# Down-projection passes of a fused GLA and MLP kernel: two of a round's three new column passes begin with a step by sums, and the last round has one more

## The chip, the cores and the metric

The kernel runs on one core of a Trainium2 chip. The time is that of one execution on the device, in microseconds (us), taken as the median of several runs. A lower time is better. One further execution is recorded by the hardware profiler, and the rows quoted here come from that one.

## The reference, cut to what matters

The trunk has one layer: a chunked gated linear attention (GLA) with a residual, then an MLP with squared ReLU and a residual, then a final RMSNorm. There are 256 tokens, a model width of 2048 and a hidden width of 8192, all in float32. The change touches the MLP alone:

```
h = h + gla_mixer(rmsnorm(h))
a = relu(rmsnorm(h) @ w_up)          # 256 x 2048 @ 2048 x 8192
h = h + (a * a) @ w_down             # 256 x 8192 @ 8192 x 2048
out = rmsnorm(h) * final_norm
```

## The kernel before

**Precision.** TensorE multiplies fp32r operands. Every float32 operand is split into two: `hi` is the rounded copy, made on ScalarE (ACT, `copy_hi`, L118), and `lo` is the rest, made on VectorE (DVE, a subtraction, L131, L154 or L943). A block product is three matmuls: hi by hi, hi by lo and lo by hi.

**The MLP.** The 8192 hidden rows are worked through in eight rounds `m` (0 to 7) of 1024. In a round, `up` makes 1024 hidden activations, and `down` multiplies them with the matching rows of `w_down`, in column groups `g` of 512 (four of them; the last round has only groups 0 and 1 here, and the other half of its columns is left to the loop at the end of the kernel). One column group in one round is a *column pass*, and a pass has four steps `kp` of 256 rows. `order_of` reverses the order of the groups each round, so the first pass of a round goes on with the group that ended the round before, and its accumulators stay where they are. The other three passes of a round are new column passes: the code calls them `fresh`.

**Two ways of a step.** A down step is a 2 by 2 by 2 product of blocks (two halves of the tokens, two of the 256 rows, two of the 512 columns). The *direct* way makes all 8 block products, 24 matmuls of 256 columns, into two accumulators, B32 and BX4. The way *by sums* (Strassen's, in Winograd's form) makes 7 block products, 21 matmuls, into four accumulators, P16, B32, P57 and BX4. It needs sums of weight blocks: three additions on DVE (L914) into `work`, one more `hi` (two copies of 128x512, L118) and one more `lo` of 128x1024 (L943), in slots of their own; of the weights themselves only three of four blocks are split (128x768 in place of 128x1024). It also needs sums of the activations, S1 to S4, which `forms` (L801) makes and `form_parts` (L811, L812) splits. `by_sums(m, g, kp)` says which way a step goes; `ways_of` collects over all groups which of the two a `kp` needs, and so how much `forms` and `form_parts` make.

**Accumulators and banks.** There are eight PSUM banks. A down pass holds four, an up half-round two, and when one up half-round follows another, the old pair is released only when DVE has normalised it (`normalized`, L786, called by `start`). Between passes an accumulator lives in SBUF: P16 and P57 in `sums`, B32 and BX4 in `h`. `begin(k, g)` takes a bank and copies the home into it; `settle(k)` copies the former pass's bank to its home and releases it; both are ACT copies of 128x512 (`copy_end`, L827). At the end of a pass, `ahead` begins B32 and BX4 of the next one in the two free banks. A fresh pass makes its step 0 the direct way, which needs only those two. P16 is settled and begun in step `first` (its first step by sums, step 1), P57 after that step's first products, and B32 and BX4 of the former pass are settled at the step's end.

**Order of the work.** The instructions are issued alternately: half an up step, half a down step. One up step and one down step together are called a *unit* below; a round has 16, so unit 0 to 3 is its first pass and units 4, 8 and 12 begin the fresh ones. `up` runs 18 steps ahead. The order is fixed on all three engines: `in_order` chains TensorE's products; on ACT each `copy_hi` and `copy_end` follows the one before it (L116 to L118, L823 to L827); on DVE the additions follow the newest `lo`, and a `lo` follows the newest additions. In a unit by sums ACT's order is: `hi` of the down weights, `hi` of the up weights, two `hi` of the sums. DVE's is: `lo` of the down weights, the additions, `lo` of the up weights, `lo` of the sums. The work on activations (`normalized`, `forms`, `form_parts`) is put in between by `piece`, one closure after each up step. There are five `hi` and `lo` slots and six raw weight tiles (`slots`, `raw_tile`).

Of the kernel before, what the change touches and what calls it, by code (L numbers as in the profile page):

```python
# [68 lines left out]
def tile_gla_mlp(ctx, tc, x, xt, cols, w_vg, w_in, w_gate, w_out, w_up, w_down, final_norm, out):  # L69
# [12 lines left out]
    def psum_bank(i, name="acc"):  # L82
        return psum.tile([P, 512], F32, tag=f"b{i}", name=name)
# [19 lines left out]
    def flush():  # L103
        while side:
            side.popleft()()
# [6 lines left out]
    def copy_hi(to, raw):  # L112
        with ExitStack() as order:
            if last_end[0]:
                order.enter_context(tc.issue_after(last_end[0]))
            if ordered[0]:  # L116
                order.enter_context(tc.issue_after(last_hi[0].ins))
            last_hi[0] = nc.scalar.copy(to, raw)  # L118
# [102 lines left out]
    g1 = lambda kt: colt[:, kt : kt + 1]  # L221
# [265 lines left out]
    at = big.tile([P, 2, HEADS, 3 * P + 64], F32R, tag="C", name="at")  # L487
# [179 lines left out]
    def order_of(m):  # L667

        return range(GROUPS)[:: 1 if m % 2 else -1]

    def by_sums(m, g, kp):

        if m == ROUNDS - 1:
            return g < 2 and kp == 2
        if m == ROUNDS - 2 and g == order_of(m)[-1]:
            return kp == 1
        return kp > 0 or m > 0 and g == order_of(m)[0]


    LEAD = KT + 2  # L680
# [16 lines left out]
    def matmul(o, x, w, first, last):  # L697
        newest[0] = nc.tensor.matmul(o, x, w, start=first, stop=last, skip_group_check=True).ins  # L698
# [123 lines left out]
    def copy_end(to, src):  # L822

        with tc.issue_after(last_hi[0].ins), ExitStack() as order:
            if last_end[0]:
                order.enter_context(tc.issue_after(last_end[0]))
            last_end[0] = nc.scalar.copy(to, src).ins  # L827
# [8 lines left out]
    P16, B32, P57, BX4 = range(4)  # L836

    def home(k, g):
        if k in (P16, P57):
            return sums[g][:, 1:3] if k == P16 else sums[g][:, 0::3]  # L840
        return h[:, k // 2, g * GT : (g + 1) * GT].rearrange("p (f s) -> p f s", f=2)
# [3 lines left out]
    def begin(k, g):  # L845
        i = free.popleft()
        bank = psum_bank(i)
        if k in (B32, BX4) or g in begun:
            copy_end(two(bank), home(k, g))
            used.add(bank.name)  # L850
        return i, bank
# [9 lines left out]
    def settle(*ks):  # L861

        for k in ks:
            late.pop(k, lambda: None)()

    def down(passes):

        ahead = pending = None
        units = 0
        for n, (m, g) in enumerate(passes):
            fresh = not n or passes[n - 1][1] != g
            if fresh:
                banks = ahead or {k: begin(k, g) for k in (B32, BX4)}
                if m == ROUNDS - 1:
                    flush()
            ends = n + 1 == len(passes) or passes[n + 1][1] != g
            first = min(kp for kp in range(KP) if by_sums(m, g, kp)) if fresh else None  # L880
            for kp in range(KP):
                last = ends and kp == KP - 1
                by_parts = by_sums(m, g, kp)

                def products(n, these, w, banks=banks, last=last):

                    with in_order():
                        for k, o, a, c in these:
                            bank = banks[k][1]
                            for x in a[: 2 - n]:  # L890
                                for d in range(0, c.stop - c.start, T):
                                    matmul(
                                        bank[:, o + d : o + d + T], x, w[n][:, c.start + d : c.start + d + T],
                                        bank.name not in used, last and n == 1,
                                    )
                                    used.add(bank.name)

                raw = raw_tile()[:, : 2 * GT]
                c0 = m * MR + 2 * kp * P
                src = w_down[c0 : c0 + 2 * P, g * GT : (g + 1) * GT].rearrange("(i p) c -> p i c", p=P)  # L900
                last_load[0] = nc.sync.dma_start(out=raw.rearrange("p (i c) -> p i c", i=2), in_=src)
                w = parts(raw, 2 * GT, slots(), [(T * by_parts, 2 * GT)])
                if fresh and kp == first:
                    settle(P16)
                    banks[P16] = begin(P16, g)
                at = lambda f, m=m, kp=kp: stationary(m, kp, f)
                block = lambda i, n=1: slice(i * T, (i + n) * T)
                if by_parts:
                    these = (P16, 0, at(A11), block(1)), (B32, T, at(A12), block(3)), (B32, 0, at(S4), block(2))
                    wk = work[:, n_sums[0] % 2]  # L910
                    n_sums[0] += 1
                    u = wk.rearrange("p (f s) -> p f s", f=4)
                    raw = raw.rearrange("p (f s) -> p f s", f=4)
                    add = lambda o, x, y: nc.vector.tensor_tensor(o, x, y, op=ALU.add)  # L914

                    with tc.issue_after(last_lo[0].ins):
                        add(u[:, :2], raw[:, :1].to_broadcast([P, 2, T]), raw[:, 1:3])
                        add(u[:, 2], u[:, 0], raw[:, 2])
                        last_sum[0] = add(u[:, 3], u[:, 2], raw[:, 3]).ins
                else:  # L920
                    these = [
                        (k, 0, at(f[i]), block(2 * i, 2))
                        for i in range(2) for k, f in ((B32, (A11, A12)), (BX4, (A21, A22)))
                    ]
                for part in range(2):
                    products(part, these, w)
                if pending:
                    for _ in pending:
                        pass
                    pending = None  # L930
                yield
                if fresh and kp == first:
                    settle(P57)
                    banks[P57] = begin(P57, g)

                def of_sums(wk=wk if by_parts else None, products=products, at=at):


                    to = slots()
                    for c in (0, GT):  # L940
                        copy_hi(to[0][:, c : c + GT], wk[:, c : c + GT])
                    with tc.issue_after(last_lo[0].ins):
                        last_lo[0] = nc.vector.tensor_tensor(to[1][:, :G], wk, to[0][:, :G].bitcast(F32), op=ALU.subtract)  # L943
                    early = (P57, 0, at(S1), block(0)), (P57, T, at(S3), block(1))
                    late = (P16, T, at(S2), block(2)), (BX4, T, at(A22), block(3))
                    products(0, early, to)
                    yield
                    products(0, late, to)
                    products(1, (*early, *late), to)

                alone = units + LEAD >= UPS
                if by_parts:
                    if alone:

                        pending = of_sums()
                    else:
                        rest = of_sums()
                        next(rest)
                yield
                if by_parts and not alone:  # L960
                    next(rest, None)
                units += 1
                if last:
                    if n + 1 < len(passes):
                        ahead = {k: begin(k, passes[n + 1][1]) for k in (B32, BX4)}
                    else:
                        last_banks(0)
                if fresh and kp == first:
                    settle(B32, BX4)
            if ends:  # L970

                def end(k, i, bank, g=g):
                    copy_end(home(k, g), two(bank))
                    free.append(i)

                late.update({k: lambda k=k, end=end, of=banks[k]: end(k, *of) for k in range(4)})
                begun.add(g)
                if m == ROUNDS - 1 or m == ROUNDS - 2 and g > 1:
                    late[BX4] = lambda f=late[BX4], g=g: (f(), side.extend(combine(g)))
# [15 lines left out]
    passes = [(m, g) for m in range(ROUNDS) for g in order_of(m) if m < ROUNDS - 1 or g < 2]  # L995
# [4 lines left out]
    for _ in down(passes):  # L1000
        next(steps, None)
# [34 lines left out]
    for kt in range(KL):  # L1036
        k = kt - KL + ROOM
# [87 lines left out]
```

## Time and profile before

| | |
|---|---|
| median of 3 runs | 1058.89 us (1058.55 to 1059.53) |
| profiled execution, its own time | 1059.51 us |
| its span | 1057.5 us, so 2.0 us lie around the span |
| TensorE (PE) busy | 1048.8 us, 9160 matmuls |
| DVE busy | 822.9 us |
| ACT busy | 693.7 us |
| a round from unit 4 to the next round's unit 4 (618.27 to 700.97) | 82.70 us: PE 82.70, DVE 76.05, ACT 62.35 |

A busy time is a union over an engine's instructions. Matmuls are pipelined, so one lasts 276 ns in the rows while the next starts about 113 ns later. DVE instructions overlap by about 0.08 us, so the distance between two starts, not the duration, is what one costs. In a timeline row the columns are start, length, engine, line, operation, names, shapes and count; brackets hold the idle time before it and what ended that.

### The profile page before, as it was taken

The page shows a single profiled execution, that of the slowest core. Times are in us where ns is not written, and L with a number is a line of the kernel's source. Part 1 is how long each engine was busy: PE and PEld are TensorE (multiplying, and loading weights), DVE is VectorE, ACT ScalarE, POOL GpSimd, SP SyncE. Part 2 cuts the span into 40 slices and gives each one's busy share as a digit, 9 for nine tenths or more (in the row PEclk, how much of TensorE's full clock was granted, in tenths as well). Part 3 has the DMA queues.
Part 4 walks back from the last instruction along what each step waited for, and adds up shares of the span by engine and source line. Part 5 has one row for each costly group of instructions (what it writes and reads, how often), then busy time and mean ns, then how long its engine had stood idle before and what let it go on. Part 6 is the DMA issues. An engine that isn't in the chain of part 4 may idle for free.

```text
span 1057.5 us, 22374 instructions
## 1 busy us (share of the span) xinstructions
PE 1048.8 (99%) x9160; PEld 1048.2 (99%) x9160; DVE 822.9 (78%) x1131; ACT 693.7 (66%) x1001; POOL 12.8 (1%) x39
## 2 busy tenths in 40 slices
PE   9999999999999999999999999999999999999997
PEld 9999999999999999999999999999999999999997
DVE  5768645656455565889989998999999998998986
ACT  5785444546454455667678678777777777777784
POOL 0000000000000000000000000000000000000000
PEclk9999999999999999999999999999999999999999
DMA  9957665556656666566666666665666665666672
GB/s 340 328 163 216 190 195 158 160 154 179 190 178 184 192 182 186 162 193 218 190 209 196 204 206 194 210 209 184 226 208 196 205 215 185 218 196 203 201 229 111
DMA packets 94791, 210.48 MB, mean 199 GB/s; under 512 B 6704, under 2 KB 7344, under 8 KB 94560
## 3 DMA queue, kind: packets, MB, share of 16 engines
q1 hardware_dynamic: 94016, 207.38, 62.5%
q8 instruction: 72, 1.18, 0.5%
q10 hardware_dynamic: 672, 1.66, 0.4%
q14 instruction: 31, 0.25, 0.1%
HBM read 206.92 MB, written 2.10 MB: 198 GB/s over the span
## 4 chain that ended last, share of the span: by engine, by line
PE 96%; DMA 2%; issue 1%; ACT 0%; SPq 0%; DVE 0%; POOLq 0%; POOL 0%; DVEq 0%; ACTq 0%
PE up L698 33%; PE acc L698 28%; PE acc L165 25%; PE acc L205 6%; PE aux L205 2%; DMA raw<-in_w_vg 1%; PE aux L165 1%; PE aux L568 1%; DMA zz<-in_xt 1%; PE aux L496 1%; SPq L157 0%; ACT sqf L1012 0%; DVE lo L131 0%; ACT hi L118 0%; PE acc L397 0%
## 5 line engine op out<-in xcount | busy, mean ns | idle before, releaser
L118 ACT CAST hi<-raw 128x1024 fp32r<-128x1024 f32 (+3 forms) x386 | 374.2, 991 | 180.8 <-PE acc L165 108.5
L131 DVE TENSOR_TENSOR lo<-raw,hi 128x1024 fp32r<-128x1024 f32 (+3 forms) x226 | 247.9, 1098 | 133.5 <-ACT hi L118 132.2
L698 PE MATMUL acc<-hi,act 128*128 128x256 f32 x1740 | 245.7, 276 | 0.0
L698 PE MATMUL up<-hl,hi 128*128 128x256 f32 x1024 | 239.4, 276 | 0.0
L698 PE MATMUL up<-hh,hi 128*128 128x256 f32 x1024 | 239.3, 276 | 0.0
L154 DVE TENSOR_TENSOR lo<-raw,hi 128x1024 fp32r<-128x1024 f32 x160 | 195.0, 1220 | 39.3 <-ACT hi L118 36.9
L698 PEld LDWEIGHTS acc<-hi,act 128*128 128x128 f32 x1740 | 219.4, 188 | 0.0
L698 PEld LDWEIGHTS up<-hl,hi 128*128 128x128 f32 x1024 | 192.3, 188 | 0.0
L698 PEld LDWEIGHTS up<-hh,hi 128*128 128x128 f32 x1024 | 192.3, 188 | 0.0
L118 ACT CAST hi<-work 128x512 fp32r<-128x512 f32 x180 | 109.6, 622 | 93.3 <-DVE work L914 91.1
L698 PE MATMUL up<-hh,lo 128*128 128x256 f32 x1024 | 137.4, 276 | 0.0
L698 PE MATMUL acc<-lo,act 128*128 128x256 f32 x870 | 132.8, 276 | 0.0
L698 PEld LDWEIGHTS up<-hh,lo 128*128 128x128 f32 x1024 | 126.1, 188 | 0.0
L943 DVE TENSOR_TENSOR lo<-work,hi 128x1024 fp32r<-128x1024 f32 x90 | 109.8, 1220 | 14.5 <-ACT hi L118 14.4
L698 PEld LDWEIGHTS acc<-lo,act 128*128 128x128 f32 x870 | 114.2, 188 | 0.0
L165 PE MATMUL acc<-hi,xA 128*128 128x256 f32 (+1 forms) x736 | 105.4, 281 | 0.5 <-ACT hi L118 0.5
L165 PEld LDWEIGHTS acc<-hi,xA 128*128 128x128 f32 x736 | 94.4, 189 | 0.7 <-ACT hi L118 0.7
L914 DVE TENSOR_TENSOR work<-work,raw 128x256 f32<-128x256 f32 x180 | 76.1, 423 | 3.9
L914 DVE TENSOR_TENSOR work<-raw 128x512 f32<-128x512 f32 x90 | 61.6, 684 | 0.0
L165 PE MATMUL acc<-lo,xA 128*128 128x256 f32 (+1 forms) x368 | 58.6, 279 | 0.1
L165 PEld LDWEIGHTS acc<-lo,xA 128*128 128x128 f32 x368 | 49.9, 189 | 0.3 <-DVE lo L131 0.3
L205 PE MATMUL acc<-xA,hi 128*128 128x256 f32 x288 | 49.2, 276 | 0.0
(158 smaller groups left out, 1145.1 us busy)
## 6 DMA issues: line engine op xcount, KB each, us to landing
raw<-in_w_up SPq DMA_DIRECT2D x128, 512.0 KB, 4.7
raw<-in_w_down SPq DMA_DIRECT2D x128, 512.0 KB, 4.2
raw<-in_w_in SPq DMA_DIRECT2D x80, 512.0 KB, 3.9
raw<-in_w_out SPq DMA_DIRECT2D x32, 512.0 KB, 3.8
raw<-in_w_vg SPq DMA_DIRECT2D x14, 520.0 KB, 8.4
h<-in_x SPq DMA_DIRECT2D x4, 512.0 KB, 8.7
out<-hf SPq DMA_DIRECT2D x5, 256.0 KB, 3.9
zz<-in_xt SPq DMA_DIRECT2D x3, 384.0 KB, 8.2
```

Of the source, the lines that this page charges most:

```text
L118: last_hi[0] = nc.scalar.copy(to, raw)
L131: last_lo[0] = nc.vector.tensor_tensor(lo[:, s], raw[:, s], hi[:, s].bitcast(F32), op=ALU.subtract)
L154: last_lo[0] = nc.vector.tensor_tensor(to[1], dst, to[0].bitcast(F32), op=ALU.subtract)
L165: nc.tensor.matmul(o[:, m], x, w[:, m], start=first and c == 0, stop=last, skip_group_check=True)
L205: nc.tensor.matmul(o, u[:, i, s], m, start=kt == 0 and n == 0 and j % 2 == 0, stop=kt == KT - 1 and n == 2, skip_group_check=True,)
L496: nc.tensor.matmul(o, kab[:, k[0], c0 + c, k[1] : k[1] + P], q(qt[:, c0 + c]), start=c == 0, stop=c == 1)
L568: nc.tensor.transpose(b[:, o + t * P : o + (t + 1) * P], src[:, t, kt * P : (kt + 1) * P], ident)
L698: newest[0] = nc.tensor.matmul(o, x, w, start=first, stop=last, skip_group_check=True).ins
L914: add = lambda o, x, y: nc.vector.tensor_tensor(o, x, y, op=ALU.add)
L943: last_lo[0] = nc.vector.tensor_tensor(to[1][:, :G], wk, to[0][:, :G].bitcast(F32), op=ALU.subtract)
```

## The change

Fresh passes that are second or fourth in a round's order (`i in (1, 3)`, units 4 and 12) now begin with a step by sums, in rounds 0 to 5, and in round 6 the second one only (its fourth pass keeps its own rule). That is 13 steps. In the last round, group 0's step 3 goes by sums too: 14 steps in all. For these passes `quick` is true. `ahead` begins B32 and P16 in place of B32 and BX4. In step 0 the former pass's B32 is settled after the split of the down weights, and P57 is begun in its place; after the `hi` copies of step 0's sums the former P57 is settled and BX4 begun. In step 1 the former P16 is settled after the split, and the former BX4 after the `hi` copies of the sums. The number of bank copies is the same as before. Third passes (unit 8) are as before. By `ways_of`, the activations of step 0 of round 0 and of step 3 of round 7 get all eight forms, where before they had four.

```diff
     def by_sums(m, g, kp):
 
         if m == ROUNDS - 1:
-            return g < 2 and kp == 2
+            return (g, kp) in ((0, 2), (0, 3), (1, 2))
         if m == ROUNDS - 2 and g == order_of(m)[-1]:
             return kp == 1
-        return kp > 0 or m > 0 and g == order_of(m)[0]
+        i = order_of(m).index(g)
+        return kp > 0 or i in (1, 3) or m > 0 and i == 0
...
         ahead = pending = None
+        quick = False
         units = 0
...
             first = min(kp for kp in range(KP) if by_sums(m, g, kp)) if fresh else None
+
+            if fresh:
+                quick = first == 0
...
                 w = parts(raw, 2 * GT, slots(), [(T * by_parts, 2 * GT)])
-                if fresh and kp == first:
+                if fresh and quick and kp < 2:
+                    settle((B32, P16)[kp])
+                    if kp == 0:
+                        banks[P57] = begin(P57, g)
+                elif fresh and kp == first:
                     settle(P16)
                     banks[P16] = begin(P16, g)
...
                 yield
-                if fresh and kp == first:
+                if fresh and kp == first and not quick:
                     settle(P57)
                     banks[P57] = begin(P57, g)
 
-                def of_sums(wk=wk if by_parts else None, products=products, at=at):
+                def of_sums(wk=wk if by_parts else None, products=products, at=at, kp=kp, banks=banks, quick=fresh and quick, g=g):
                     to = slots()
                     for c in (0, GT):
                         copy_hi(to[0][:, c : c + GT], wk[:, c : c + GT])
+                    if quick and kp == 0:
+                        settle(P57)
+                        banks[BX4] = begin(BX4, g)
+                    elif quick and kp == 1:
+                        settle(BX4)
                     with tc.issue_after(last_lo[0].ins):
                         last_lo[0] = nc.vector.tensor_tensor(to[1][:, :G], wk, to[0][:, :G].bitcast(F32), op=ALU.subtract)
...
                     if n + 1 < len(passes):
-                        ahead = {k: begin(k, passes[n + 1][1]) for k in (B32, BX4)}
+                        m1, g1 = passes[n + 1]
+                        ahead = {k: begin(k, g1) for k in (B32, P16 if by_sums(m1, g1, 0) else BX4)}
                     else:
                         last_banks(0)
-                if fresh and kp == first:
+                if fresh and kp == first and not quick:
                     settle(B32, BX4)
```

## The prediction

> **What bounds the kernel now.** I read the page first, then the busy times of one round, then the timelines of DVE, ACT and PE through that round.
>
> ```profile
> span 1057.5 us, 22374 instructions
> ...
> PE 1048.8 (99%) x9160; PEld 1048.2 (99%) x9160; DVE 822.9 (78%) x1131; ACT 693.7 (66%) x1001; POOL 12.8 (1%) x39
> ```
>
> TensorE is the bound: 99% of the span. The average of DVE, 78%, hides its rounds. One round, from unit 4 to the next unit 4 (columns: stretch, length, then busy time of PE, PEld, DVE, ACT, POOL, clock, DMA share, GB/s), and the end of the kernel, for later:
>
> ```profile
> 618.27:700.97 82.70, 82.70 (x732) 82.70 (x731) 76.05 (x105) 62.35 (x90) 0.00 (x0) 1.00 0.64 205
> ...
> 1040.00:1057.00 17.00, 10.36 (x92) 10.16 (x90) 10.04 (x26) 6.92 (x19) 1.10 (x2) 0.93 0.34 125
> ```
>
> PE never waits in the round, and DVE is idle for only 82.70 - 76.05 = 6.65 us of it. The change takes work from PE and gives work to DVE, so those 6.65 us are the matter. In DVE's timeline, units 4 (direct), 5 and the start of 6:
>
> ```profile
> 616.60 1.23 DVE L131 TENSOR_TENSOR lo<-raw,hi 128x1024 fp32r<-128x1024 f32 x1 [0.41 <-ACT hi L118]
> 617.74 1.22 DVE L154 TENSOR_TENSOR lo<-raw,hi 128x1024 fp32r<-128x1024 f32 x1
> 618.88 0.95 DVE L131 TENSOR_TENSOR lo<-raw,hi 128x768 fp32r<-128x768 f32 x1
> 619.75 0.68 DVE L914 TENSOR_TENSOR work<-raw 128x512 f32<-128x512 f32 x1
> ...
> 621.33 1.23 DVE L154 TENSOR_TENSOR lo<-raw,hi 128x1024 fp32r<-128x1024 f32 x1
> 623.51 1.23 DVE L943 TENSOR_TENSOR lo<-work,hi 128x1024 fp32r<-128x1024 f32 x1 [0.95 <-ACT hi L118]
> 625.21 0.96 DVE L131 TENSOR_TENSOR lo<-raw,hi 128x768 fp32r<-128x768 f32 x1 [0.48 <-ACT hi L118]
> ...
> 629.88 0.95 DVE L131 TENSOR_TENSOR lo<-raw,hi 128x768 fp32r<-128x768 f32 x1
> ```
>
> A direct unit costs DVE 618.88 - 616.60 = 2.28 us; a unit by sums, run without a wait, 629.88 - 625.21 = 4.67 us. Its parts are the down split 0.87 (619.75 - 618.88), the additions 1.58 (621.33 - 619.75), and two splits of 1.14 (617.74 - 616.60). PE in units by sums:
>
> ```profile
> 627.82 1.07 PE L698 MATMUL up<-hh,lo 128*128 128x256 f32 x8
> ...
> 632.92 1.07 PE L698 MATMUL up<-hh,lo 128*128 128x256 f32 x8
> ```
>
> That is 5.10 us for 24 + 21 = 45 matmuls, 0.1133 us each; a direct unit is 48, 5.44 us. So DVE gains 0.43 us on PE in a unit by sums, and 3.16 in a direct one. The direct units are where DVE's lead is won back after the activation work.
>
> **The lead.** How far DVE is ahead of PE at unit 3, just before the fresh pass:
>
> ```profile
> 694.73 1.08 DVE L812 TENSOR_TENSOR act<-work,act 128x896 fp32r<-128x896 f32 x1
> ...
> 696.53 1.22 DVE L154 TENSOR_TENSOR lo<-raw,hi 128x1024 fp32r<-128x1024 f32 x1
> ...
> 699.29 1.23 DVE L131 TENSOR_TENSOR lo<-raw,hi 128x1024 fp32r<-128x1024 f32 x1 [0.41 <-ACT hi L118]
> ```
>
> ```profile
> 696.62 0.84 PE L698 MATMUL acc<-hi,act 128*128 128x256 f32 x6
> ...
> 699.90 1.07 PE L698 MATMUL up<-hh,lo 128*128 128x256 f32 x8
> ```
>
> The up split ends at 697.75 and is used at 699.90: lead 2.15. In unit 5 it ended at 622.56 for a use at 627.82: lead 5.26. The closest call is the split of the activations of step 3, `form_parts`: it ends at 695.81, and unit 3's first products read it from 696.62 on, 0.81 later. So when the up split's lead at unit 3 falls under 2.15 - 0.81 = 1.34, PE stops.
>
> **The change part by part.**
>
> *PE.* Fourteen steps lose 3 matmuls each: 42 x 0.1133 = **-4.8 us**, all on the bound. A full round loses two steps: 82.70 - 6 x 0.1133 = 82.02.
>
> *DVE in a round.* Two units go from direct to by sums: 2 x (4.67 - 2.28) = +4.78. DVE's round runs from the start at 616.60 to the one at 699.29, 82.69. Its waits in between are 0.95 and 0.48 (above), the 0.41 at 699.29, and these:
>
> ```profile
> 634.54 1.28 DVE L786 SCALAR_TENSOR_TENSOR su<-up,work 128x512 f32<-128x512 f32 x2
> 637.46 1.23 DVE L131 TENSOR_TENSOR lo<-raw,hi 128x1024 fp32r<-128x1024 f32 x1 [1.64 <-ACT hi L118]
> ...
> 644.33 1.23 DVE L943 TENSOR_TENSOR lo<-work,hi 128x1024 fp32r<-128x1024 f32 x1 [0.49 <-ACT hi L118]
> ...
> 646.98 0.96 DVE L131 TENSOR_TENSOR lo<-raw,hi 128x768 fp32r<-128x768 f32 x1 [0.28 <-ACT hi L118]
> ...
> 658.19 1.23 DVE L131 TENSOR_TENSOR lo<-raw,hi 128x1024 fp32r<-128x1024 f32 x1 [0.41 <-ACT hi L118]
> ...
> 665.07 1.23 DVE L943 TENSOR_TENSOR lo<-work,hi 128x1024 fp32r<-128x1024 f32 x1 [0.95 <-ACT hi L118]
> 666.77 0.96 DVE L131 TENSOR_TENSOR lo<-raw,hi 128x768 fp32r<-128x768 f32 x1 [0.48 <-ACT hi L118]
> ```
>
> Together 6.09 in nine waits. Without a wait an instruction starts about 0.08 before the former one ends (1.22 long, 1.14 apart), so a wait costs 0.08 more than its bracket: 6.8. DVE's work is 82.69 - 6.8 = 75.9, and after the change 80.7. That leaves 1.3 us under PE's 82.02. So it decides which waits stay once DVE is late and no longer held back by PE.
>
> *The wait that stays: 1.64 at unit 8.* ACT at that place:
>
> ```profile
> 635.26 1.19 ACT L827 COPY acc<-h 128x512 f32<-128x512 f32 x2 [2.25 <-DVE su L786]
> 636.38 2.00 ACT L118 CAST hi<-raw 128x1024 fp32r<-128x1024 f32 x2
> ```
>
> ACT begins the next pass's banks, and they are the ones that DVE's `su` releases; ACT itself waited 2.25 us for DVE. Then come two copies and the cast, and DVE's next split waits for that cast. This is DVE to ACT to DVE, with PE nowhere in it: if DVE is later, the wait moves along unchanged. Unit 8 is not a quick pass, so 1.64 + 0.08 = 1.72 stay. Of the 0.57 and 0.36 behind it (0.49 and 0.28 with the 0.08), some hung on a copy that waited for PE: ACT's own starts, run on from 636.38 without that wait, save 0.37, and 0.57 is left.
>
> *The waits at quick starts (units 4 and 12).* ACT there, as it is now:
>
> ```profile
> 614.48 1.10 ACT L827 COPY acc<-h 128x512 f32<-128x512 f32 x2
> 615.52 2.73 ACT L118 CAST hi<-raw 128x1024 fp32r<-128x1024 f32 x3
> 619.10 0.59 ACT L827 COPY sums<-acc 128x512 f32<-128x512 f32 x1 [0.85 <-PE acc L698]
> 619.73 0.59 ACT L827 COPY acc<-sums 128x512 f32<-128x512 f32 x1
> 620.25 1.05 ACT L118 CAST hi<-raw 128x1024 fp32r<-128x1024 f32 x1
> ```
>
> A settle with its begin takes 1.15 us of ACT (620.25 - 619.10). In the new order, by the same starts: cast of the down weights 615.52 to 616.35, so DVE loses 0.27 against 616.11, where it could have started (616.60 - 0.41 - 0.08); its additions begin at 617.25. ACT: B32 out and P57 in to 617.4, up cast, two casts of sums to 619.4 (behind the additions), P57 out and BX4 in to 620.55, next down cast to 621.4. DVE could go on at 621.11, behind its additions and two 1.14 splits, and loses 0.30. After that ACT is ahead again. So 0.57 a quick start, where 0.41 + 0.95 + 0.48 and three times 0.08 = 2.1 stood. Bounds: 0 (all hidden) and 2.1 (as now); 0.57 is worked out from this order, so I take it. PE isn't held by the banks: BX4 is needed 37 matmuls, 4.2 us, behind the boundary at 619.0 and is in at 620.6. Uncovered, 1.15 would be paid at each of 13 starts, 15 us.
>
> *The round's sum.* 80.7 + 1.72 + 0.57 + 2 x 0.57 = 84.1 against PE's 82.02: DVE loses **2.1 us** a round, and PE must wait for it once the lead is spent.
>
> *The lead at the start.* Unit 4 of round 0 is the first quick start:
>
> ```profile
> 453.62 1.98 PE L698 MATMUL acc<-hi,act 128*128 128x256 f32 x16
> ...
> 462.43 1.07 PE L698 MATMUL up<-hh,lo 128*128 128x256 f32 x8
> ```
>
> ACT is there far enough ahead to stand at the boundary, 453.62, until PE gives P57 free. Then 1.15 for the copies, 0.83 for the cast, 0.87 + 1.58 + 1.22 on DVE: unit 5's up split ends at 459.3, for a use 74 matmuls behind the boundary, at 462.0. Lead 2.7. From there to unit 3 of round 1 is a round less units 4 and 5, which win 2 x 0.43 - 0.57 = 0.3: the lead falls by 2.1 + 0.3 = 2.4 to 0.3, and 1.34 is the least: first stall 1.0. Five more rounds (the unit 3 of rounds 2 to 6) pay 2.1 each, 10.5. Behind unit 4 of round 6 the direct steps of its last pass restore the lead. Stalls: **+11.5**.
>
> *The rest, at nothing.* Group 0's step in round 7 costs DVE 2.39 more, and its activations about 1.2 (half of an L812 and three L801); the direct units there, without up steps, cover it, and if not, 2.4 at most. The activations of round 0 fall before unit 4, where the lead stands at its cap. The change adds no DMA; the loads stand in the same order, with six raw tiles (three units, 15 us) against a DVE lag of 2.
>
> **Sum:** 1059.5 - 4.8 + 11.5 = 1066.2 for the profiled execution, which lies 0.6 over the median: **1065.6 us**.
>
> **The rivals.** *Quick starts cost nothing.* Then DVE needs 80.7 + 1.72 + 0.57 = 83.0, the lead of 2.7 lasts through the first round, and five rounds lose 1.0 each: +5.0 - 4.8, about 1059, no change. For it: the quick order hides most casts, and the starts worked out above miss by only 0.3. Against: ACT has two copies between the casts of the sums and the next down cast that weren't there.
>
> *Faster: DVE never falls behind.* If DVE's waits come to less than 1.3 a round, PE gains all 4.8: 1054.1; with the 1.72 alone a round loses 0.4, five of them 2, and it is 1056. For it: DVE's bare work does fit. Against: ACT's order, as worked out, gives 3.4. It decides at a round sum of 82.02.
>
> *The clock drops.* The one window with a clock under 1 is the last, 0.93 with 6.6 us of PE idle: 1.2 us lost of 17. Six stalls with that loss would add 7, to 1073. The Trainium skill, "TensorE: Matmul & The Clock Gate", section "HAM oscillation — how this bites in real kernels", puts the drop at idle gaps over about 3.4 us; by that rule stalls of 2.1 would cost no clock, and the trace's last window neither shows nor excludes where the limit lies.
>
> **How the numbers follow.** Two runs differ by about 0.2% (2 us) from nothing but measurement. The DVE chain has 0.60; its own range goes from quick starts of 0.27 (1.5 a round: 0.4 + 7.5 - 4.8 = +3) to quick starts of 0.85 with the 0.37 kept (3.0 a round: 1.9 + 15 - 4.8 = +12): 1062 to 1071. No change has 0.10, faster 0.22, the clock or a worse wait 0.08. The range reaches down into the faster case, to 1055.5, and up to 1071.5; about 0.2 lies outside. With the edges of these cases: faster 0.23, same 0.11, slower 0.66.
>
> **What would show it.** Matmuls 9160 - 42 = 9118; DVE's rounds near 81 busy; rounds of about 84 from round 2 on; PE idle of 1 to 2.5 us ahead of unit 3's accumulating products, released by L812 or a `lo` of DVE; the 1.64 still ahead of unit 8's split. Wrong would be: rounds of 82.0 without PE idle, or PE waiting for bank copies at the quick starts.

## The result and the profile after

The changed kernel takes 1068.48 us (median of 4 runs, 1067.39 to 1069.25) against 1058.78 before: a ratio of 1.0089, 95% interval 1.0077 to 1.0101. It is 9.7 us **slower**. The forecast was 1065.6, range 1055.5 to 1071.5. Its profiled execution took 1068.25 us, with a span of 1066.2, 8.7 above the span before. All line numbers from L671 on are shifted: L699 here is L698 before, L813 is L812, L923 is L914, L957 is L943, L787 is L786, L828 is L827.

From the page after: the counts and busy times that answer to the first lines of the prediction.

```profile
span 1066.2 us, 22388 instructions
...
PE 1052.5 (99%) x9118; PEld 1049.7 (98%) x9118; DVE 855.9 (80%) x1193; ACT 705.2 (66%) x1029; POOL 12.8 (1%) x39
```

TensorE has the 42 matmuls less (9160 to 9118) and is still "99% busy", with *more* busy time than before. DVE has 33 us more. From the busy times of one stretch, unit 8 to the next round's unit 8 (columns as in the prediction):

```profile
639.81:723.93 84.12, 82.86 (x726) 82.56 (x725) 80.39 (x112) 63.88 (x95) 0.00 (x0) 1.00 0.63 200
```

DVE is busy for 80.4 of 84.1 us, and the granted clock is 1.00. In the chain of work that ended last (start, length, what), the long piece of each round is unit 8's direct step. It marks the rounds:

```profile
473.51 3.63 PE acc L699 x32
...
555.53 3.63 PE acc L699 x32
...
639.81 3.63 PE acc L699 x32
...
723.93 3.63 PE acc L699 x32
...
807.96 3.63 PE acc L699 x32
...
892.17 3.63 PE acc L699 x32
```

The distances are 82.02, then 84.28, 84.12, 84.03 and 84.21. The first round still lives on the lead and has just the matmuls that it should; all others have the 84.1 that the prediction gave to DVE and ACT. DVE's waits in the first of the longer rounds, from its timeline (unit 4, at 618.04 and 623.08, has the same two as unit 12):

```profile
555.94 1.23 DVE L131 TENSOR_TENSOR lo<-raw,hi 128x1024 fp32r<-128x1024 f32 x1 [1.64 <-ACT hi L118]
...
562.41 1.23 DVE L957 TENSOR_TENSOR lo<-work,hi 128x1024 fp32r<-128x1024 f32 x1
...
565.05 0.96 DVE L131 TENSOR_TENSOR lo<-raw,hi 128x768 fp32r<-128x768 f32 x1 [0.28 <-ACT hi L118]
...
576.03 0.96 DVE L131 TENSOR_TENSOR lo<-raw,hi 128x768 fp32r<-128x768 f32 x1 [0.20 <-ACT hi L118]
...
581.08 0.96 DVE L131 TENSOR_TENSOR lo<-raw,hi 128x768 fp32r<-128x768 f32 x1 [0.29 <-ACT hi L118]
```

The 1.64 at unit 8 stands to the hundredth, the 0.28 behind it too; the 0.49 is gone; the quick start at unit 12 has 0.20 and 0.29, where 0.19 and 0.22 were worked out (0.27 and 0.30 with the 0.08). The six waits of the round come to 2.90, 3.4 with the 0.08 each; 84.1 less that is 80.7, the work that was predicted. TensorE's waits, all of them (waiter, releaser, total, times, longest):

```profile
PE acc L699 <- DVE act L813: 4.2, 5, 1.3
PE aux L231 <- DVE ones L228: 1.0, 1, 1.0
PE acc L699 <- ACT hi L118: 0.8, 2, 0.6
PE acc L165 <- ACT hi L118: 0.5, 1, 0.5
```

The first line is the predicted releaser, the split of step 3's activations ahead of unit 3. But its 4.2 us are less than half of what the five rounds lost (10.7, below). The rest is in gaps that no row shows, since a matmul's 276 ns cover them, and in TensorE's pace. Two pairs of successive units by sums, 45 matmuls each, from its timeline:

```profile
585.90 1.10 PE L699 MATMUL up<-hh,lo 128*128 128x256 f32 x8
...
591.20 1.10 PE L699 MATMUL up<-hh,lo 128*128 128x256 f32 x8
...
690.08 1.07 PE L699 MATMUL up<-hh,lo 128*128 128x256 f32 x8
...
695.18 1.14 PE L699 MATMUL up<-hh,lo 128*128 128x256 f32 x8
...
697.16 0.50 PE L699 MATMUL acc<-hi,act 128*128 128x256 f32 x2
698.92 0.74 PE L699 MATMUL acc<-hi,act 128*128 128x256 f32 x4 [1.26 <-DVE act L813]
```

In round 3 (690 on) a unit takes 5.10 us, 113.3 ns a matmul, and then TensorE stops for the split. From unit 13 of round 1 (586) on every unit takes 5.30, 117.8 ns a matmul, with no wait in any row until a short one at unit 3 of round 2. The round is equally long in both: DVE and ACT set it, and TensorE either stops once or goes slowly. The slower pace began at 578.1, in the quick start at unit 12 of round 1, behind a stop of 0.2 us by the starts of the matmuls, too short for a row. The product there begins 0.05 us behind the end of ACT's cast of the up weights (577.04 to 578.09), and in the new order that cast stands behind two bank copies. The pace ended at 624, in unit 4 of round 2.

So the account of the span's 8.7 us: -4.8 for the matmuls; +10.7 for five rounds (from unit 3 to unit 3: 84.14, 84.09, 84.06, 84.21 and 84.33, against 82.02 each); about +1.0 at unit 8 of round 6 and +1.6 in the last round (below). That is 8.5; the MLP's first matmul already stands 0.2 later than before.

### The profile page after: what moved, and what is told of

The parts are those of the page before. It is cut to its first block, busy times and chain, and to the rows that moved or that the text cites. A ratio compares the mean times of both kernels' runs of the same rounds, so it can differ in the third digit from the quotient of the medians.

```text
span 1066.2 us, 22388 instructions
## 1 busy us (share of the span) xinstructions
PE 1052.5 (99%) x9118; PEld 1049.7 (98%) x9118; DVE 855.9 (80%) x1193; ACT 705.2 (66%) x1029; POOL 12.8 (1%) x39
## 4 chain that ended last, share of the span: by engine, by line
PE 88%; DVE 7%; DMA 2%; issue 2%; ACT 1%; SPq 0%; POOLq 0%; POOL 0%; DVEq 0%; ACTq 0%
PE up L699 29%; PE acc L165 25%; PE acc L699 24%; PE acc L205 6%; PE aux L205 2%; DVE lo L154 1%; DVE lo L131 1%; DVE work L923 1%; DMA raw<-in_w_vg 1%; DVE lo L957 1%; DVE act L813 1%; PE aux L165 1%; PE aux L568 1%; DMA zz<-in_xt 1%; PE aux L496 1%
## 5 line engine op out<-in xcount | busy, mean ns | idle before, releaser
L131 DVE TENSOR_TENSOR lo<-raw,hi 128x1024 fp32r<-128x1024 f32 (+3 forms) x226 | 244.3, 1082 | 128.5 <-ACT hi L118 127.3
L699 PE MATMUL acc<-hi,act 128*128 128x256 f32 x1712 | 250.2, 277 | 5.0 <-DVE act L813 4.2
L699 PE MATMUL up<-hh,hi 128*128 128x256 f32 x1024 | 240.9, 277 | 0.0
L699 PE MATMUL up<-hl,hi 128*128 128x256 f32 x1024 | 240.8, 277 | 0.0
L699 PEld LDWEIGHTS acc<-hi,act 128*128 128x128 f32 x1712 | 219.8, 188 | 6.8 <-DVE act L813 5.2
L118 ACT CAST hi<-work 128x512 fp32r<-128x512 f32 x208 | 127.7, 622 | 119.8 <-DVE work L923 100.2
L699 PEld LDWEIGHTS up<-hh,hi 128*128 128x128 f32 x1024 | 192.3, 188 | 0.2
L699 PEld LDWEIGHTS up<-hl,hi 128*128 128x128 f32 x1024 | 192.2, 188 | 0.0
L699 PE MATMUL up<-hh,lo 128*128 128x256 f32 x1024 | 138.2, 277 | 0.0
L699 PE MATMUL acc<-lo,act 128*128 128x256 f32 x856 | 134.3, 277 | 0.0
L957 DVE TENSOR_TENSOR lo<-work,hi 128x1024 fp32r<-128x1024 f32 x104 | 126.8, 1219 | 1.5 <-ACT hi L118 1.1
L699 PEld LDWEIGHTS up<-hh,lo 128*128 128x128 f32 x1024 | 126.6, 188 | 0.1
L699 PEld LDWEIGHTS acc<-lo,act 128*128 128x128 f32 x856 | 114.3, 188 | 0.0
L923 DVE TENSOR_TENSOR work<-work,raw 128x256 f32<-128x256 f32 x208 | 88.0, 423 | 4.9
L923 DVE TENSOR_TENSOR work<-raw 128x512 f32<-128x512 f32 x104 | 71.2, 684 | 0.0
```

Source lines behind the costliest of these rows:

```text
L131: last_lo[0] = nc.vector.tensor_tensor(lo[:, s], raw[:, s], hi[:, s].bitcast(F32), op=ALU.subtract)
```

## Experiments

Theory A is the prediction's: DVE and ACT need 84.1 us for a round, and TensorE stops once the lead is spent. Rival B: each quick start (a fresh pass that begins by sums) has a price of its own at TensorE (copies into the banks), 1.1 us each if all is laid to it. Rival C: the late split of the activations, a single dependency, is all of it. Ratios are to the kernel before on the same chip, with 95% intervals. The edits of `ends` change the list of closures that `piece` runs, one a unit: a closure that stands one place further ahead in it runs a unit earlier.

### Only the second passes begin by sums (e1)

```diff
-        return kp > 0 or i in (1, 3) or m > 0 and i == 0
+        return kp > 0 or i == 1 or m > 0 and i == 0
```

The last round's rule is that of the kernel before, here and in all that follow except e3, e4 and e5.

> Only second passes (unit 4, rounds 0 to 6) begin by sums; fourth passes and the last round are as before. Theory A (VectorE and ScalarE need 84.1 us for a round and TensorE 82.0; the lead is spent): one direct start more per round gives VectorE its slack back at unit 12, the lead at unit 11 falls from 2.1 to about 1.5 and is restored, no stall: 7 x 3 matmuls x 0.1133 = 2.4 us less, 1056.4. Rival B (each quick start costs TensorE a wait for bank copies; 9.7 us more plus the 4.8 saved over 13 starts is 1.1 each): 7 x (1.1 - 0.34) = +5.4, 1064.2. Rival C (the late split of step 3's activations, needed at unit 3, is all of it): as A here.

Measured: 1060.37 us, ratio 1.0013 (1.0004 to 1.0022). No theory has it. Up to unit 8 of round 6, though, A is right: no row shows a wait in the rounds, and unit 7 of round 6 stands 2.8 us earlier than before (966.06 against 968.82), 0.4 of which is there before the MLP. Behind that, from TensorE's timeline:

```profile
966.06 1.07 PE L699 MATMUL up<-hh,lo 128*128 128x256 f32 x8
...
968.28 2.16 PE L699 MATMUL acc<-hi,act 128*128 128x256 f32 x16 [0.24 <-ACT hi L118]
...
973.10 1.10 PE L699 MATMUL up<-hh,lo 128*128 128x256 f32 x8
...
982.76 1.10 PE L699 MATMUL up<-hh,lo 128*128 128x256 f32 x8
988.06 1.10 PE L699 MATMUL up<-hh,lo 128*128 128x256 f32 x8
```

A wait for the `hi` that stands behind the bank copies of unit 8, about 0.7 us in all (7.04 from 966.06 to 973.10, where the kernel before takes 6.35 over the same unit), and from then on the slower pace, 5.30 a unit, to the end: some 660 matmuls by 4.5 ns, 2.9 us. 0.7 + 2.9 - 2.4 = +1.2, where the medians are 1.4 apart.

### Only the fourth passes (e2)

```diff
-        return kp > 0 or i in (1, 3) or m > 0 and i == 0
+        return kp > 0 or i == 3 or m > 0 and i == 0
```

> Only fourth passes (unit 12, rounds 0 to 5) begin by sums. Theory A: the lead of 2.1 at unit 11 is not restored at unit 12 and falls by 1.2 until unit 3, to 0.9, where 1.34 is needed: a stall of about 0.4 in each of six rounds, 2.6, less 6 x 0.34 = 2.0: about 1059.4, no change; unit 4, direct again, restores the lead, so stalls don't grow. Rival B: 6 x 0.76 = +4.6, 1063.4. In either, the gain per start is smaller than with second passes under A, the same under B.

Measured: 1063.11 us, ratio 1.0038 (1.0026 to 1.0051). That is rival B's number, but not its mechanism. TensorE loses 0.5 us at unit 3 of rounds 2, 4 and 5 and 0.8 in round 6, together 2.3, where A had 0.4 in each of six; nothing is lost at the quick starts themselves. From unit 3 of round 2 to unit 4 of round 3 it runs at 5.30 a unit, 3.4 us more. With -2.0 for the matmuls and some 0.6 of slower pace behind the other stops, that is 4.3 against the measured 4.2. The size of a stop is about right under A; what A lacked is the pace.

### The activation work a unit earlier (e3)

```diff
-        return [nothing, start, lambda: make(0), lambda: (split(0), make(1)), lambda: split(1)]
+        return [nothing, lambda: (start(), make(0)), lambda: (split(0), make(1)), lambda: split(1)]
```

> The changed kernel, with the work on a finished up half-round in four closures in place of five: the bank release stays where it is, the activation forms and their splits come one unit earlier, so that the split needed at unit 3 has 5 us more. Theory A: VectorE's round is as long as before, 84.1, so the stall rate stays at 2.1 a round; only the least lead falls from 1.34 to about 0.2, which is gained once: 1068.5 - 1.2 = 1067.3, and TensorE now waits for something else (a lo or hi). Rival C: the stalls go, 1068.5 - 10.7 = 1057.8. Rival B: no change, 1068.5.

Measured: 1067.75 us, ratio 1.0084 (1.0071 to 1.0098), A's 1067.3. Rival C falls: with the late split out of the way, TensorE waits for other things, and the rounds stay 84 us. All its waits:

```profile
PE acc L699 <- ACT hi L118: 3.4, 7, 0.7
PE acc L699 <- DVE lo L957: 1.9, 4, 0.5
PE aux L231 <- DVE ones L228: 1.0, 1, 1.0
```

### The banks released a unit earlier (e4)

```diff
-        return [nothing, start, lambda: make(0), lambda: (split(0), make(1)), lambda: split(1)]
+        return [start, nothing, lambda: make(0), lambda: (split(0), make(1)), lambda: split(1)]
```

> The changed kernel, with the bank release of a finished up half-round one unit earlier (the empty closure behind it in place of ahead of it); forms and splits stay. It takes away VectorE's wait of 1.64 ahead of unit 8's split, as the banks are free a unit before ScalarE fills them; what such a start costs without it is 0.41 by the direct starts of the kernel before. Theory A: 1.2 us less a round, 0.9 lost per round in place of 2.1; with the lead that round 0 keeps, stalls of about 3 in place of 10.7: 1068.5 - 7.5 = 1061. Rivals B and C: nothing changes at the quick starts or in the time of the split, 1068.5.

Measured: 1060.76 us, ratio 1.0016 (1.0008 to 1.0025); A had 1061, the rivals 1068.5. One line that touches no quick start takes back 7.7 of the 9.7 us. The five rounds from unit 3 to unit 3 take 82.9 us each (the last 83.3), where A's 84.1 less 1.2 is 82.9. Part of the hit is luck, though: the five rounds lose 4.7 where A had 3, and the wait at unit 8 of round 6 goes as well, about 1.0, which A did not count. In DVE's timeline the wait at unit 8 is what a direct start costs without the banks, and the release (L787) stands 6 us ahead of it:

```profile
630.63 1.28 DVE L787 SCALAR_TENSOR_TENSOR su<-up,work 128x512 f32<-128x512 f32 x2
...
636.98 1.23 DVE L131 TENSOR_TENSOR lo<-raw,hi 128x1024 fp32r<-128x1024 f32 x1 [0.41 <-ACT hi L118]
```

### The last round's extra step alone (e5)

```diff
-            return g < 2 and kp == 2
+            return (g, kp) in ((0, 2), (0, 3), (1, 2))
```

This is the kernel before with that one line.

> The kernel before with only the last round's extra step by sums. In the changed kernel the last 28 us run at the slower of TensorE's two paces, 117.8 ns a matmul in place of 113.3, behind a 0.27 us wait for a hi. If the extra step is the cause: -0.34 + 0.27 + 28 / 0.1178 x 0.0045 = +1.0, about 1059.9. If the step is covered, as the prediction had it: -0.3, 1058.6.

Measured: 1059.54 us, ratio 1.0007 (0.9998 to 1.0016), between the two numbers. The profiled execution (1058.85) has the 0.27 us wait for a `hi`, which costs TensorE 0.5 us by the starts of its matmuls where the step saves 0.34, and it keeps the faster pace behind it. In the profiles of the changed kernel (at 1031.90), of e3 and of e4 the same wait is followed by the slower pace to the end. The step is no gain. Whether some of the eleven runs had the slower pace isn't shown: seven took 1058.7 to 1059.8 us and four 1060.4 to 1060.7, but the spans of the four (1057.5 to 1058.0) don't stand apart from the others (1056.6 to 1057.7); the four have 2.4 to 3.0 us around the span, the others 1.9 to 2.2.

### Second passes with the earlier release (e6)

This is e1 and e4 together.

> The kernel with second passes only (e1), with the bank release one unit earlier (as in e4). In e1 nothing stalled up to round 6's third pass; there TensorE waited 0.7 us for a hi behind the banks, and the slower pace from there to the end, some 680 matmuls x 4.5 ns = 3.1 us, took the gain back. If that is so, the earlier release takes away this one wait, no pace changes, and the whole 2.4 us is left: 1056.5. If a quick start itself costs TensorE something, 1060 stays.

Measured: 1056.66 us, ratio 0.9979 (0.9970 to 0.9988). The wait in round 6 is gone, and so is the slower pace; 2.3 of the 2.4 us are there. These seven quick starts cost TensorE nothing, and rival B falls.

### Fourth passes in every second round (e7)

```diff
-        return kp > 0 or i == 1 or m > 0 and i == 0
+        return kp > 0 or i == 1 or i == 3 and m in (0, 2, 4) or m > 0 and i == 0
```

(against e6.)

> As e6, and fourth passes by sums in rounds 0, 2 and 4 as well: ten steps. In e4 a round with both quick starts loses 0.7 us of lead (1.41 behind a stall to 0.70 ahead of the next); in e1 a round with the second alone ends at 2.15. So every second round may have both: 2.15 - 0.7 = 1.45 against the least of 1.34, and the next round restores it. No stall: 10 x 0.34 = 3.4 less, 1055.5. If the lead is not what decides, three more starts with both passes by sums give three stalls of 0.7 and the slower pace behind each: 1059 or more.

Measured: 1056.78 us, ratio 0.9981 (0.9972 to 0.9990), no better than e6. From 2.17 at unit 3 of round 2 the lead falls not by 0.7 but by 1.2, as it falls faster from a higher start; TensorE loses 0.47 us at unit 3 of rounds 3 and 5 and runs slowly for most of a unit behind it.

### A second turn of the pace (e8)

In the kernels so far the slower pace ended, where it ended, in unit 4 of a round. There `up` has its step 6, whose weights lie in a shifted layout (the second half 16 columns further on) and whose last products run in the other order (`even`). This is e1 with one more such step, a unit behind the wait in round 6:

```diff
-                even = ((6,), (0,))[q] if m == 0 else (6,) if q == 0 else ()
+                even = ((6,), (0,))[q] if m == 0 else (6,) if q == 0 else (3,) if m == ROUNDS - 1 else ()
```

> The kernel with second passes only (e1), with the up weights of one more step (step 3 of the last half-round, a unit behind the wait in round 6) in the shifted layout and order that the seventh step of every round has. In all runs so far the slower pace ends, where it ends, at that step. If that layout is what ends it, the slower pace of the last 80 us goes after about 10 us: 1060.4 - 2.7 = 1057.7. If not, 1060.4 stays, or the faster pace is lost elsewhere.

Measured: 1057.68 us, ratio 0.9986 (0.9977 to 0.9995). TensorE's timeline has the same wait as e1, then two units at the slower pace, then the faster one:

```profile
968.89 2.15 PE L699 MATMUL acc<-hi,act 128*128 128x256 f32 x16 [0.21 <-ACT hi L118]
...
973.71 1.10 PE L699 MATMUL up<-hh,lo 128*128 128x256 f32 x8
...
983.18 1.07 PE L699 MATMUL up<-hh,lo 128*128 128x256 f32 x8
988.28 1.07 PE L699 MATMUL up<-hh,lo 128*128 128x256 f32 x8
```

### The release alone (e9)

The edit of e4, made to the kernel before.

> The kernel before, with the earlier bank release alone. There TensorE never waits in the rounds, so 1.2 us more slack of VectorE a round buys nothing: 1058.9, no change. If the release were a gain by itself, e6 would owe it its 2.3 us and this kernel would be near 1056.7.

Measured: 1059.00 us, ratio 1.0000 (0.9991 to 1.0009). DVE's slack is worth nothing where TensorE doesn't need it.

### Alternate rounds, both a unit earlier (e10)

e7 with `return [start, lambda: make(0), lambda: (split(0), make(1)), lambda: split(1)]`.

> As e7 (second passes in all rounds, fourth in 0, 2 and 4), with the release and the activation work both a unit earlier. In e7 the lead falls to about 0.9 at unit 3 of rounds 3 and 5, and TensorE waits 0.5 us for the late split of the activations, then runs at the slower pace for some 9 us. With the split 5 us earlier the least lead is 0.2 to 0.5: no stall, all ten steps gained: 1055.5. Against: in e3, with that work in one unit with the release, TensorE waited 2 us at unit 8; if that came from the work and not from the release, 1058 or more.

Measured: **1055.65 us**, ratio 0.9967 (0.9955 to 0.9980), the best version: 0.33%, 3.4 us, faster than before, which is what the ten steps are worth. From its page:

```profile
PE 1045.1 (99%) x9130; PEld 1044.9 (99%) x9130; DVE 847.5 (80%) x1174; ACT 699.0 (66%) x1021; POOL 12.8 (1%) x39
```

and TensorE's waits, of which none lies in the MLP:

```profile
PE aux L231 <- DVE ones L228: 1.0, 1, 1.0
```

### All thirteen quick starts, both a unit earlier (e11)

> All 13 quick starts, the last round as before, release and activation work a unit earlier. A round loses 0.7 of lead (e4), of which 1.36 are there at unit 3 of round 1, 0.2 to 0.5 needed: stalls of 5 x 0.7 - 1.0 = 2.5, some slower pace behind them, 13 x 0.34 = 4.4 saved: about 1057.5, better than before but not than e6.

The closures are those of e10. Measured: 1061.16 us, ratio 1.0019 (1.0010 to 1.0028). The rounds go about as expected (0.6 to 1.0 lost around unit 3 of each of rounds 3 to 6), but in round 6 the wait at unit 8 is back (6.83 in place of 6.35) and behind it 5.30 a unit to the end, as in e1: 0.5 + 2.9 = 3.4 us that were not expected.

## Why the prediction was right, and where not

*Sign and cause* held: slower, by DVE and ACT, with TensorE's rounds at 84.1 (predicted 84.1), through the lead at unit 3, at the releaser that was named. e4 shows the cause: it takes away the one wait that the prediction called the one that stays, the rounds become shorter by just the 1.2 us that this wait costs beyond a direct start's 0.41, and 7.7 of the 9.7 us come back.

*The waits at the quick starts*, 0.57 a start, were worked out from ACT's order alone: 0.20 and 0.29 in the rows, 0.65 with the 0.08 each. *The wait that stays* is as measured. *The round's sum* (2.1 a round) is too, but by a little luck: two quick starts have 0.16 more than worked out, and behind unit 8 stands 0.36 where 0.57 was left.

*The lead at the start.* Unit 5 of round 0 was to have 2.7, and unit 3 of round 1 0.3 with a first stop of 1.0. From DVE's and TensorE's timelines after:

```profile
458.16 1.22 DVE L154 TENSOR_TENSOR lo<-raw,hi 128x1024 fp32r<-128x1024 f32 x1
...
531.43 1.22 DVE L154 TENSOR_TENSOR lo<-raw,hi 128x1024 fp32r<-128x1024 f32 x1
```

```profile
462.24 1.07 PE L699 MATMUL up<-hh,lo 128*128 128x256 f32 x8
...
533.98 1.07 PE L699 MATMUL up<-hh,lo 128*128 128x256 f32 x8
```

The leads are 2.86 and 1.33. The second is just the least of 1.34 that was read from before, and there is no stop. This step failed: it charged round 0 with a full round's 2.1, and round 0 lost about 1.2. By the code, a column group of round 0 has no sums yet to bring back into a bank, and the prediction didn't take those copies out; that this is the whole difference was not tried. The term was +1.0 and measured 0.

*"The rest, at nothing"* failed by 2.6 us. Behind unit 4 of round 6 the direct steps were to restore the lead, but unit 8 of that round comes first, and its `hi` behind the banks was late by 0.57; and the last round's extra step was not covered: two `hi` more on ACT give the wait of 0.27 at 1031.90, and the pace does the rest. The 1.6 of the last round lie within the 2.4 that the prediction named as the most. So 10.7 + 2.6 stands where 11.5 stood, 1.8 of the 2.0 us by which the profiled execution was missed (1066.2 forecast, 1068.25 measured). The median was 2.9 us higher than forecast: the profiled execution was put 0.6 above it, as before, and lies 0.2 below it.

*The clock* kept to 1.00 in the round's row (639.81 to 723.93), in which TensorE loses 1.9 us around its stop, so that rival is out. The Trainium skill ("TensorE: Matmul & The Clock Gate", "HAM oscillation — how this bites in real kernels") puts the loss of clock at idle gaps over about 3.4 us. By that rule these stops cost no clock, and the 1.00 agrees. A loss of pace at a full clock was in no rival.

*"PE idle ahead of unit 3"* was right in rounds 3, 4 and 6 and hardly visible in rounds 2 and 5, where most of the same 2.1 us are spread over the matmuls. One sign of being wrong did show in small: at unit 12 of rounds 1 and 4 TensorE stopped for 0.1 to 0.2 us for a cast behind bank copies, and its slower pace began there. It did not change the length of those rounds (84.14 and 84.21).

## What to carry to other kernels

Taking work from the bound engine is worth something only if the engine that gets the work has that much left *in its round, with its waits counted*; here 1.3 us of room met 3.4 us of waits. Ask of each wait whether it hangs on the bound engine (it shrinks when the others fall behind) or is a loop among the others (it stays), and cut the loop first: e4's one line was worth 7.7 us on the changed kernel and nothing on the one before. And a lead is a store that some rounds must refill: spending it in every second round (e10) gained 3.4 us, and spending it in every round with the same closures (e11) lost 2.1.

## What the runs showed of the hardware

In these runs' MLP, TensorE has two paces for the same matmul of 256 columns, at a granted clock of 1.00: 113.3 ns (5.10 for 45) and 117.8 ns (5.30), 4% apart. It fell to the slower one behind a stop as short as 0.1 us by the starts (unit 12 of round 4 after) and stayed there for some 90 us in e1 and e2, without a single idle row. Not every wait does this: e3 has a stop of 0.4 to 1.0 us at unit 8 of rounds 1 to 6, and only the one in round 5 was followed by the slower pace. In e8 one step of weights in a shifted layout and order brought the faster pace back; the same step, once a round, ended it elsewhere, except in round 2 of e2. What the two paces are is open: the shifted layout and the reversed order were not tried apart. The slower pace stands in the kernel before as well, in earlier stages, there too at a clock of 1.00 (245 to 260); from its chain of work:

```profile
250.21 5.66 PE acc L165 x48
```

5.66 / 48 is 117.9 ns.
